# A tuned LoRA kernel on one core: the first two stores wait for the fourth group's projection

## The chip, the core and the metric

The kernel runs on one core of one Trainium2 chip. The core has five engines that run side by side and meet only through semaphores: TensorE (PE, matrix products, with its weight loads as PEld), VectorE (DVE), ScalarE (ACT), GpSimd (POOL) and SyncE (SP). SyncE computes nothing here; it issues every DMA of this kernel. The DMAs are carried out by 16 DMA engines of the core. The metric is the device time of one launch in microseconds (us).

## What is computed

```python
def reference(x, A, B, scale):
    lora = np.matmul(np.matmul(x, A), B)
    return (x + scale * lora).astype(np.float32)
```

x is 16 x 512 x 768 in float32 (25.2 MB), A is 768 x 16, B is 16 x 768, scale is 0.5. The output has the shape of x. So 25.2 MB are read and 25.2 MB are written, and two thin matrix products stand between.

## The kernel before

The 8192 rows of x are cut into 64 tiles of 128 rows. PARTS = [8, 8, 16, 16, 16] (L14) puts the tiles into five parts; inside a part each SBUF partition holds consecutive rows, so that a partition's piece of a transfer is one contiguous row of 6 to 48 KB. The SBUF tensor x_sb has room for 48 tiles, the first four parts; part 4 reuses the places of parts 0 and 1 (L103, modulo ROOM).

The work goes in 8 groups of 8 tiles (GROUP). For a group g:

- ScalarE and GpSimd each cast half of the group to float16, x_sb to xn (L182). For g over 0 they first wait for the load and for s_taken to reach g (L181).
- VectorE transposes xn to xt in one instruction (L238).
- TensorE projects: 24 matmuls into ps_yt (L269). The second of them adds one to s_taken (L277), and no one takes from that counter: its value says how many groups TensorE has begun to project.
- ScalarE spreads the projected values, times scale, into y_bd (L226).
- TensorE multiplies with B into one of two PSUM buffers lora_ps, two tiles at a time ("pairs", four in a group, L290).
- VectorE adds lora_ps to x_sb in place (L243), pair by pair. The sum that completes a store's tiles adds one to s_sum; any other frees its PSUM buffer by s_free.

The order of the instructions on each engine is written out by hand, one function per engine. TensorE interleaves the second product of group g with the projection of group g+1.

SyncE's list sets the order of all DMAs (L135 to L170): loads 0 and 1, the small A and B, loads 2 to 5 (all of them at once, with no wait in between), then the stores of parts 0 and 1, each after a wait for its sum, then loads 6 and 7, each after a wait for one of these stores to land (they fill the same SBUF places), then stores 2, 3 and 4, each after its sum. When SyncE has seen a sum that completes a store, it also frees the PSUM buffer of the group's last pair in VectorE's place (L145). The loads are

```python
LOADS = [
    (0, 0, 2), (0, 2, 6), (1, 0, 8), (2, 0, 8), (2, 8, 8), (3, 0, 16), (4, 0, 8), (4, 8, 8)
]
```

as (part, first tile, tiles). The first six bring 48 tiles, 18.9 MB; load 5 alone is 6 MB. The stores are one per part.

Of the kernel before, what the change touches and what calls it, by code (L numbers as in the profile page):

```python
# [28 lines left out]
def kernel(  # L29
# [53 lines left out]
    def sem(name):  # L83
        sems.append(nc.alloc_semaphore(name))
        return sems[-1]
# [10 lines left out]
    def memory(t2, i, s, n):  # L96
        S = PARTS[i]
        return t2[ds(parts[i], S * P), :].rearrange("(p s) d -> p s d", s=S)[:, ds(s, n), :]

    def held(i, s, n):  # L100
        return tiles(where.index((i, s)), n)

    def tiles(t, n):  # L103
        return x_all[:, ds(t % ROOM, n), :]
# [14 lines left out]
    s_first, s_narrow, s_turned, s_taken = sem("s_first"), sem("s_narrow"), sem("s_turned"), sem("s_taken")  # L119
# [8 lines left out]
    STORES = [(0, 0, 8), (1, 0, 8), (2, 0, 16), (3, 0, 16), (4, 0, 16)]  # L128
# [6 lines left out]
    def on_sync(e):  # L135
        def load(k):
            ld = LOADS[k]
            e.dma_start(out=held(*ld), in_=memory(x2, *ld)).then_inc(s_load[k], 16)  # L138

        def store(k, done):  # L140
            st = STORES[k]
            e.wait_ge(s_sum, k + 1)
            if STORED[k] + 1 < NG:

                e.sem_inc(s_free[PAIRS - 1], 1)  # L145
            e.dma_start(out=memory(out2, *st), in_=held(*st)).then_inc(done, 16)

        load(0)
        load(1)
        e.wait_ge(s_ready, 1)  # L150
        blocks = A.rearrange("(c e) r -> c (e r)", e=64)
        for c in range(SETS):
            e.dma_start(
                out=a_rows[c : SET * SET : SET, :], in_=blocks[ds(c * SET, SET), :]
            ).then_inc(s_a, 16)
        e.wait_ge(s_brows, 1)
        e.dma_start(out=b_rows[0 : R * APART : APART, :], in_=B).then_inc(s_b, 16)
        for k in range(2, len(LOADS) - 2):
            load(k)

        for p in range(2, PAIRS):
            e.sem_inc(s_free[p], 1)
        store(0, s_out0)
        store(1, s_out1)
        e.wait_ge(s_out0, 16)
        load(len(LOADS) - 2)
        e.wait_ge(s_out1, 16)
        load(len(LOADS) - 1)
        for k in range(2, len(STORES)):
            store(k, s_out)  # L170

    here = set()
# [88 lines left out]
    def on_tensor(e):  # L261
# [57 lines left out]
        for p in range(PAIRS):  # L319
            raised(p)  # L320

    on_sync(nc.sync)
    on_gpsimd(nc.gpsimd)
    on_scalar(nc.scalar)
# [46 lines left out]
```

## Time and profile before

| what | value |
|---|---|
| median of 3 runs | 124.05 us (123.84 to 124.35) |
| the profiled execution | 124.01 us, of which the span is 122.2 us |
| DMA queue | one, 1928 packets, 50.43 MB, 96.7% of 16 engines' span |
| VectorE busy | 81.7 us (67%) |
| TensorE busy | 52.3 us (43%) |
| ScalarE, GpSimd busy | 37.4 us, 28.4 us |
| first store issued, landed | 32.82 us, 55.59 us |
| second store issued | 42.74 us |
| load 6 issued, landed | 55.61 us, 70.20 us |
| last store issued | 101.2 us |

The span runs from the first to the last instruction; the measured time holds a little more around it. The slices of the page cut the span in 40 parts of 3.05 us, and a digit is the busy share in tenths. "SPq" rows are SyncE's instructions, and a DMA row of the chain of waits reaches from the issue to the landing, so that time in the queue is in it. A DMA moves one packet per partition here, 128 in all and 8 for each DMA engine, and after its packets each DMA engine writes a small mark (4 bytes) that raises the semaphore; the packet counts of a window split by size, so the marks can be told from the data.

### The profile page before, as it was taken

The page shows a single profiled execution, that of the slowest core. Times are in us where ns is not written, and L with a number is a line of the kernel's source. Part 1 is how long each engine was busy: PE and PEld are TensorE (multiplying, and loading weights), DVE is VectorE, ACT ScalarE, POOL GpSimd, SP SyncE. Part 2 cuts the span into 40 slices and gives each one's busy share as a digit, 9 for nine tenths or more (in the row PEclk, how much of TensorE's full clock was granted, in tenths as well). Part 3 has the DMA queues.
Part 4 walks back from the last instruction along what each step waited for, and adds up shares of the span by engine and source line. Part 5 has one row for each costly group of instructions (what it writes and reads, how often), then busy time and mean ns, then how long its engine had stood idle before and what let it go on. Part 6 is the DMA issues. An engine that isn't in the chain of part 4 may idle for free.

```text
span 122.2 us, 885 instructions
## 1 busy us (share of the span) xinstructions
PE 52.3 (43%) x322; PEld 30.4 (25%) x322; DVE 81.7 (67%) x42; ACT 37.4 (31%) x43; POOL 28.4 (23%) x24
## 2 busy tenths in 40 slices
PE   0000239487457547746745735974674340000000
PEld 0000026253233424424423322642442110000000
DVE  0002850599999999999999979999995991000000
ACT  4002938526408311835340093553004000000000
POOL 7631638026008001705300080440000000000000
PEclk9999999999999999999999996799999955555555
DMA  3999999999998996999999999999899899899890
GB/s 60 420 434 428 451 426 410 459 418 418 483 515 354 418 515 257 467 410 434 442 410 451 426 418 491 426 499 418 370 499 418 370 499 434 354 515 434 386 467 0
DMA packets 1928, 50.43 MB, mean 413 GB/s; under 512 B 236, under 2 KB 236, under 8 KB 392
## 3 DMA queue, kind: packets, MB, share of 16 engines
q1 hardware_dynamic: 1928, 50.43, 96.7%
HBM read 25.26 MB, written 25.17 MB: 413 GB/s over the span
## 4 chain that ended last, share of the span: by engine, by line
DMA 39%; DVE 28%; PE 7%; ACT 3%; issue 3%; POOL 2%; SPq 0%; DVEq 0%
DMA x_sb<-in_x_dram 20%; DMA out_dram<-x_sb 19%; DVE x_sb L243 18%; DVE xt L238 10%; PE ps_yt L269 5%; ACT xn L182 3%; POOL xn L182 2%; PE lora_ps L290 1%; SPq L138 0%; SPq L366 0%; DVEq L256 0%; SPq L145 0%; SPq L133 0%
## 5 line engine op out<-in xcount | busy, mean ns | idle before, releaser
L243 DVE TENSOR_TENSOR x_sb<-x_sb,lora_ps 128x1536 f32<-128x1536 f32 x32 | 53.7, 1733 | 1.4 <-PE lora_ps L290 1.4
L290 PE MATMUL lora_ps<-b_mm,y_bd 128*128 128x512 f16 (+1 forms) x128 | 26.5, 343 | 22.7 <-issue 15.0
L182 ACT CAST xn<-x_sb 128x3072 f16<-128x3072 f32 (+1 forms) x9 | 23.4, 2609 | 36.8 <-DMA x_sb<-in_x_dram 24.2
L238 DVE STREAM_TRANSPOSE xt<-xn 128x3072 f32<-128x3072 f32 (+1 forms) x9 | 27.0, 3004 | 6.7 <-PE ps_yt L269 5.5
L269 PE MATMUL ps_yt<-xt,w_bd 128*128 128x256 f16 x192 | 26.5, 291 | 11.5 <-DVE xt L238 11.5
L182 POOL CAST xn<-x_sb 128x3072 f16<-128x3072 f32 (+1 forms) x8 | 20.7, 2586 | 45.9 <-DMA x_sb<-in_x_dram 23.3
L269 PEld LDWEIGHTS ps_yt<-xt,w_bd 128*128 128x128 f16 x192 | 19.2, 102 | 19.5 <-issue 14.6
L290 PEld LDWEIGHTS lora_ps<-b_mm,y_bd 128*128 128x128 f16 x128 | 11.1, 100 | 36.0 <-issue 18.1
L226 ACT ACTIVATE y_bd<-ps_yt 32x256 f16<-32x256 f32 x32 | 12.0, 374 | 18.3 <-PE ps_yt L269 18.0
L231 DVE STREAM_TRANSPOSE a_t<-a_rows 32x1024 f32<-32x1024 f32 x1 | 1.9, 1945 | 11.4 <-DMA a_rows<-in_A_dram 11.4
L302 PE MATMUL lora_ps<-b_half,pick 128*128 128x512 f16 (+1 forms) x2 | 0.8, 504 | 12.6 <-POOL b_half L200 12.6
L302 PEld LDWEIGHTS lora_ps<-b_half,pick 128*128 128x128 f16 x2 | 0.1, 102 | 12.6 <-issue 12.6
L208 POOL COPY w_bd<-w_one 32x384 f16<-32x384 f16 x4 | 2.0, 500 | 0.2
L200 POOL CAST b_half<-b_rows 128x768 f16<-128x768 f32 x1 | 0.8, 827 | 4.4 <-DMA b_rows<-in_B_dram 4.4
L182 ACT ACT_TABLE_LOAD x1 | 1.3, 1283 | 0.9 <-SPq L133 0.9
L190 POOL MEMSET w_bd<- 128x1536 f32 x1 | 1.4, 1372 | 0.0
L202 POOL CAST w_one<-a_t 32x384 f16<-32x384 f32 x1 | 0.9, 852 | 0.9 <-DVE a_t L231 0.9
L187 POOL MEMSET a_rows<- 32x1024 f32 x1 | 0.9, 941 | 0.5 <-SPq L133 0.5
L219 ACT CAST b_mm<-lora_ps 128x768 f16<-128x768 f32 x1 | 0.8, 798 | 0.0
L188 POOL MEMSET b_rows<- 128x768 f32 x1 | 0.7, 727 | 0.0
L191 POOL MEMSET y_bd<- 128x512 f32 x1 | 0.5, 514 | 0.0
L193 POOL TENSOR_SCALAR_AFFINE_SELECT pick<-pick 128x128 f16<-128x128 f16 x1 | 0.3, 298 | 0.0
(5 smaller groups left out, 0.6 us busy)
## 6 DMA issues: line engine op xcount, KB each, us to landing
out_dram<-x_sb SPq DMA_DIRECT2D x3, 6144.0 KB, 23.6
x_sb<-in_x_dram SPq DMA_DIRECT2D x5, 3072.0 KB, 14.6
x_sb<-in_x_dram SPq DMA_DIRECT2D x1, 6144.0 KB, 42.2
out_dram<-x_sb SPq DMA_DIRECT2D x2, 3072.0 KB, 21.5
x_sb<-in_x_dram SPq DMA_DIRECT2D x1, 2304.0 KB, 9.9
x_sb<-in_x_dram SPq DMA_DIRECT2D x1, 768.0 KB, 4.7
a_rows<-in_A_dram SPq DMA_DIRECT2D x3, 16.0 KB
b_rows<-in_B_dram SPq DMA_DIRECT2D x1, 48.0 KB, 7.5
```

What stands on the lines that cost most here:

```text
L182: ins = copy(out=xn[:, ds(first, n), :], in_=tiles(t, n))
L187: e.memset(a_rows[0:Q], 0.0).then_inc(s_ready, 1)
L190: e.memset(w_bd.rearrange("p c k m -> p (c k m)").bitcast(fp32), 0.0)
L202: e.tensor_copy(out=w_one.rearrange("i (c e) k r -> i c e (k r)", c=SETS), in_=a_t[0:Q].rearrange("i k r (e c) -> i c e (k r)", c=SET)[:, ...
L208: e.tensor_copy(out=w_bd[ds(b * Q, Q), :, :, ds(b * Q, R)], in_=w_one).then_inc(s_w, 1)
L226: last = e.mul(out=y_bd[q, :, q], in_=y_ps[q, :, :], mul=sc)
L231: e.transpose(out=a_t[0:Q].rearrange("i k r c -> i (k r) c"), in_=a_rows[0:Q].rearrange("c (i k r) -> c (k r) i", k=2, r=R),).then_inc(s_r ...
L238: return e.transpose(out=ts[0], in_=ts[1])
L243: ins = e.tensor_tensor(out=xs, in0=xs, in1=lora[p % 2], op=mybir.AluOpType.add)
L269: mm = e.matmul(y_ps, w_bd[:, c, k, :], xv[:, :, c, :, k], start=(m == 0), stop=(m == MMS - 1),)
L290: mms.append(e.matmul(t[:, k, ds(n0, w)], y_bd[:, 2 * p + k, :], b_mm[:, ds(n0, w)], start=True, stop=True,))
L302: last = e.matmul(lora[0][:, 0, ds(n0, w)], pick.rearrange("p b r -> p (b r)"), b_half[:, ds(n0, w)], start=True, stop=True,)
```

## The change

SyncE's helper for a store is split in two: `summed(k)` waits for the sum and frees the PSUM buffer, `store(k)` only issues. For stores 0 and 1 the two waits come first, then a new wait for s_taken to reach 4, that is for the second projecting matmul of the fourth group (g = 3), and then both stores are issued one after the other. The later stores keep their order: wait, free, issue. No other engine's instructions change.

```diff
+        def summed(k):
+            e.wait_ge(s_sum, k + 1)
+            if STORED[k] + 1 < NG:
+
+                e.sem_inc(s_free[PAIRS - 1], 1)
+
         def store(k, done):
             st = STORES[k]
-            e.wait_ge(s_sum, k + 1)
-            if STORED[k] + 1 < NG:
-
-                e.sem_inc(s_free[PAIRS - 1], 1)
             e.dma_start(out=memory(out2, *st), in_=held(*st)).then_inc(done, 16)
 
         load(0)
...
         for p in range(2, PAIRS):
             e.sem_inc(s_free[p], 1)
+        summed(0)
+        summed(1)
+
+
+        e.wait_ge(s_taken, 4)
         store(0, s_out0)
         store(1, s_out1)
         e.wait_ge(s_out0, 16)
...
         load(len(LOADS) - 1)
         for k in range(2, len(STORES)):
+            summed(k)
             store(k, s_out)
```

More of the change, by code (lines that the diff above doesn't have):

```diff
@@ L138, in load @@
             e.dma_start(out=held(*ld), in_=memory(x2, *ld)).then_inc(s_load[k], 16)
-        def store(k, done):
-            st = STORES[k]
+        def summed(k):
             e.wait_ge(s_sum, k + 1)
@@ L145, in store @@
                 e.sem_inc(s_free[PAIRS - 1], 1)
+        def store(k, done):
+            st = STORES[k]
             e.dma_start(out=memory(out2, *st), in_=held(*st)).then_inc(done, 16)
```

## The prediction

> **What bounds the kernel now.** I read the page's 40 slices first, then the queues, then the chain that ended last, and last the DMA packets around the place where the stores are issued.
>
> ```profile
> DVE  0002850599999999999999979999995991000000
> ...
> DMA  3999999999998996999999999999899899899890
> ...
> q1 hardware_dynamic: 1928, 50.43, 96.7%
> ```
>
> From the second slice to the last but one the 16 DMA engines are full, and one queue carries all of it (packets, MB, share). VectorE, the busiest other engine with 67%, ends its last sum at 94.43 + 6.75 = 101.2 us, twenty before the end. So the time is the length of the DMA stream: a start, 50.43 MB at full rate, and any hole in it. Next, the chain of waits, from the first store on:
>
> ```profile
> 32.75 0.02 SPq L145
> 32.77 0.05 issue
> 32.82 22.77 DMA out_dram<-x_sb
> 55.59 0.02 issue
> 55.61 14.59 DMA x_sb<-in_x_dram
> ```
>
> The first store is issued at 32.82 and landed at 55.59, 22.8 us for 3 MB that take 7.3 at full rate. It stood in line. The packets of four short windows show where (columns: packets, MB, and the time the packets took as a share of 16 engines over the window):
>
> ```profile
> q1 hardware_dynamic: 110, 5.41, 99.8%
> ...
> q1 hardware_dynamic: 16, 0.79, 202.0%
> ...
> q1 hardware_dynamic: 16, 0.79, 242.5%
> ...
> q1 hardware_dynamic: 34, 0.44, 104.5%
> ```
>
> The first is 34.0 to 46.9 us: 110 packets of 5.41 MB are 49 KB each, the rows of the 6 MB load, and no store packet is among them although a store has been queued since 32.8 and a second since 42.7. The queue is first in, first out. The fourth is 47.0 to 47.99: 34 packets, of which that answer counts 16 under 512 B (one finishing mark per DMA engine) and the other 18 carry 24.6 KB. So each of the 16 engines ends the last load and begins the first store inside this one microsecond, at 47.0 to 48.0, with nothing lost between. The second and third are 42.9 to 43.8 and 44.7 to 45.6, the last but one and the last 49 KB packet of every engine in that load: 2.020 x 16 x 0.9 / 16 = 1.82 us each, and 2.425 x 0.9 = 2.18 us. The last packets of the load are stretched by 0.36 us on average. That is the only visible flaw of the stream after its start, and the only thing that the queued stores could be blamed for.
>
> **The change, part by part.** SP's two counter steps for group 0 and 1 (L145, at 32.75 and 42.7) stay where they were, since the new helper does them ahead of the new wait: TensorE gets lora_ps buffers as before, cost 0. The two store instructions move from 32.82 and 42.73 to behind a wait for s_taken = 4, the second projecting matmul of the fourth group. Its time:
>
> ```profile
> 36.15 0.38 PE L269 MATMUL ps_yt<-xt,w_bd 128*128 128x256 f16 x2 [1.41 <-DVE xt L238]
> 36.62 2.75 ACT L182 CAST xn<-x_sb 128x3072 f16<-128x3072 f32 x1 [3.44 <-PE ps_yt L269]
> 46.07 0.49 PE L269 MATMUL ps_yt<-xt,w_bd 128*128 128x256 f16 x3 [1.42 <-DVE xt L238]
> 48.34 2.75 ACT L182 CAST xn<-x_sb 128x3072 f16<-128x3072 f32 x1 [5.25 <-DMA x_sb<-in_x_dram]
> ```
>
> One group earlier two matmuls take 0.38 us and ScalarE's cast, which waits for the same counter, starts 0.09 later. So the counter reaches 4 at 46.07 + 0.38 = 46.45 and SP issues the first store at about 46.5, the second 0.4 later. Nothing before that time hangs on a store, so 46.07 itself stays. Behind the wait on SP stand the two stores and then the waits for them to land; SP has nothing else until 55.61.
>
> So the first store now reaches the queue when some engines have 0.5 us of load left and others 1.5. What decides is how long an issued DMA takes to its first packets in an empty queue. The trace has one such place, the first load of the kernel:
>
> ```profile
> 0.96 0.38 SPq L138 DMA_DIRECT2D x_sb<-in_x_dram  x1
> ...
> q1 hardware_dynamic: 14, 0.09, 100.3%
> ```
>
> Issued at 0.96; the second line is the window 1.9 to 2.45, with 14 first packets, the earliest starting at 1.97, and the last engines follow by about 2.5. So 1.0 to 1.55 us from issue to start. Then the packets are slow: those 14 took 1.003 x 16 x 0.55 / 14 = 0.63 us each, against 0.25 in the window 3.3 to 4.0 (45 packets, 98.8%, so 0.988 x 16 x 0.7 / 45), 0.4 us more on a first packet.
>
> The sum, engine by engine. Stores would start at 46.5 + 1.0 to 46.5 + 1.55 = 47.5 to 48.05, where they now start at 47.0 to 48.0. The end is set by the slowest engine, since each has its fixed rows: by the packets the engine that starts the first store last (47.98) also ends last (120.8). Its start moves by 48.05 - 47.98 = 0.07. Added to it is the slow beginning s. Bounds for s: nothing, if reading SBUF has none of the first load's slowness; and on the other side all of that load: its row of 4.7 us to landing is 5.69 on the clock, less 0.35 from last packet to landing (48.34 against 47.98 above) and 8 packets of 0.25, is 2.4 us from issue to an equivalent start at full rate on its slowest engine, hence 46.5 + 2.4 - 47.98 = 0.9 us in all, and s = 0.85. I take the middle, 0.45: the first load read cold from HBM, the store reads from SBUF. Sum +0.07 + 0.45 = +0.5 us.
>
> Does a hole of that size reach the end? Load 6 is issued when store 0 lands, behind store 1 with 7.4 us of packets (55.61 to 63.0), so no second hole opens; all later DMAs shift together. The cast of group 6 (at 70.25, after load 6) shifts along, VectorE ends 0.5 later, and the last store is issued at 101.7 while the store ahead of it, issued at 83.20 with the median 23.6 us to landing, holds the queue to 106.8: cover of over 2 us stays. So the hole is paid in full, once. Gain side: if the queued stores cause the 0.36 us stretch, the loads end earlier by it, but the engines then wait for the stores, which come at 47.5 anyway; group 4's cast at 48.34 would be earlier too, and VectorE does not wait for it now (it is busy without a gap from 25 to 70 us). That gain is covered: 0.
>
> The profiled run took 124.01 us around a span of 122.2; the median of three is 124.05. So 124.01 + 0.5, on the median's scale 124.55.
>
> **A rule of the Trainium skill.** The row says 1.0 us from issue to the first packet. The Trainium skill, DMA: Bandwidth & Descriptors, Specifications, gives a first-byte latency of about 0.6 us for DMAs issued by SyncE; counted from the issue that would be an estimate of a store start at 47.1, almost hidden, and 124.05 in all; the trace agrees with 0.6 only if counted from the end of the issuing instruction (0.96 + 0.38 to 1.97). The same page, Rules for kernel authors, says to issue a DMA early so that its fixed setup overlaps; that speaks against the change, and it is the hole reckoned above.
>
> **The rivals.**
> - *Clearly slower.* The stores pay the first load's whole beginning, s of 0.85 or a little more: 124.05 + 0.07 + 0.85 = 125.0. For it: the only empty queue in the trace behaved so. Against it: there 16 engines waited for cold HBM reads of 6 KB rows; here the rows are 24.6 KB in SBUF. From s of 0.55 on, it is slower by over 0.5%.
> - *Hidden anyway.* s near 0 and a start 0.4 earlier than the first load shows: most engines are still busy with load when the store's packets come. 124.05, no change. For it: 46.5 is before 47.0 for all engines. Against it: 1.0 us of latency.
> - *Faster.* One mechanism: the queued store stretches each engine's last load packet; without it the loads end 0.36 us earlier (on the engine at 47.98 even 0.8, since its packet took 2.66), and the store's packets come within 0.6 us of the issue, by 47.1 to 47.4 (the latest of the load's last packets starts at 45.6, and 45.6 + 1.82 is 47.4). Then the slowest engine gains 47.98 - 47.4 = 0.58: 123.45. It decides only from a start below 0.9 us after issue. Against it: the first load's 1.0 to 1.55.
> - *Not what it says.* At 46.5 the last load still has 0.5 to 1.5 us to go, so the stores do get queued behind loads, only briefly; and 99.8% in the window 34.0 to 46.9, with both stores waiting, shows no slowing there to win back. This caps the gain at what the last packets of the load can give back.
>
> **How the numbers follow.** Forecast +0.2 to +0.8 us around 124.55: 0.52, of which I put 0.15 above the 0.62 us that are 0.5% (about what a measurement of this kernel can tell from no change). Clearly slower, +0.8 and more: 0.25. Hidden, within 0.2 either way: 0.15. Faster: 0.08, of which 0.05 by over 0.5%, as 0.58 is its middle and short of the line. So slower 0.15 + 0.25 = 0.40, faster 0.05, same 0.55. The range goes from 123.9, which leaves out the faster cases, to 125.2, the upper bound of 125.0 and the spread of the three runs (0.2) over it; some 2 in 10 lie outside.
>
> **What would show it.** Right: SP issues the first store near 46.5; the DMA row falls below full for about half a microsecond at 47 to 48.5, and packets of 24.6 KB begin there from 47.5 on; the store lands near 56.1 instead of 55.59, and everything after it is shifted alike. The stretch step is shown by the mean of the last 49 KB packets, 2.18 us or 1.82. Wrong: if store packets begin at 47.1, or if the stores' landing moves by more than 1 us, or if the later DMAs do not shift with it.

## The result and the profile after

The changed kernel takes 125.37 us (median of 12 runs, 124.29 to 126.35) against 124.06 us of the kernel before: a ratio of 1.0096, 95% interval [1.0079, 1.0113]. It is slower by about 1%, and it has become uneven: its runs lie 2 us apart, those of before 0.5. (The ratio leaves out the one run that lies over 1.5% above the kernel's fastest.) On another occasion the same kernel took 124.61 us against 124.11, ratio 1.0037 [1.0019, 1.0054], with runs from 124.10 to 126.03. So it is slower on both occasions, but the size of the loss (1.3 and 0.5 us) is not fixed. The traced run took 125.63 us with a span of 123.8, so it is a typical one of the first twelve.

SyncE's own rows tell most of it, since load 6 is issued when store 0 has landed and load 7 when store 1 has. First the kernel before, then the changed one (start, time, engine, line, what):

```profile
55.61 7.77 SPq L138 DMA_DIRECT2D x_sb<-in_x_dram  x2
63.50 0.36 SPq L146 DMA_DIRECT2D out_dram<-x_sb  x1
```

```profile
46.37 0.82 SPq L148 DMA_DIRECT2D out_dram<-x_sb  x2
55.26 8.50 SPq L138 DMA_DIRECT2D x_sb<-in_x_dram  x2
63.89 0.37 SPq L148 DMA_DIRECT2D out_dram<-x_sb  x1
```

The stores are issued at 46.37. Store 0 has landed at 55.26, 0.35 us *earlier* than before. Store 1 has landed when the second instruction of the pair begins: 63.04 before (55.61 + 7.77 less its 0.34), 63.42 after. So between the two landings 0.73 us were lost. Store 2's row in the list of DMA issues of each kernel (KB, us from issue to landing) gives the rest:

```profile
out_dram<-x_sb SPq DMA_DIRECT2D x1, 6144.0 KB, 28.7
```

```profile
out_dram<-x_sb SPq DMA_DIRECT2D x1, 6144.0 KB, 30.0
```

It lands at 92.2 before and 93.9 after, 1.7 later. Stores 3 and 4, read in the same way (23.7 and 20.2 us after), land at 108.4 and 122.9, against 106.8 and 121.3: 1.6 later. So the change gains 0.35 us up to 55 us, loses 2 us between 55 and 94, and nothing more after that. The loss is nowhere near the place that was changed.

The packets show the two places. In the changed kernel's DMA windows (packets, MB, packet time as a share of 16 engines over the window), in order: 44.8 to 45.7, the last packets of load 5; 46.6 to 47.2; and 47.1 to 47.6, the first packets of store 0.

```profile
q1 hardware_dynamic: 16, 0.79, 202.2%
...
q1 hardware_dynamic: 12, 0.00, 1.1%
...
q1 hardware_dynamic: 22, 0.39, 187.1%
```

The last packets of load 5 take 2.022 x 0.9 = 1.82 us: the stretch of 0.36 us that they had before is gone. Then 12 engines write their mark and nothing else begins until 47.2: a pause like the one predicted, 0.2 us on average. All 16 begin store 0 between 47.2 and 47.5 (16 of the 22 packets are data), and those first packets take 1.871 x 0.5 x 16 / 16 = 0.94 us, as good as the usual 0.91. SyncE waits for the marks of all 16 engines (`wait_ge(s_out0, 16)`), and it is the last of them that gained. By the packet records they end store 0 within 0.24 us of each other, where they lay 0.95 apart before; the average engine ends it at 54.63, against 54.67 before, so it has gained next to nothing. Now the packets ahead of the two later turns: 60.9 to 61.25, the last of store 1 before load 6; then 75.4 to 76.1, the last but one of load 7 before store 2.

```profile
q1 hardware_dynamic: 16, 0.39, 469.6%
...
q1 hardware_dynamic: 16, 0.39, 224.2%
```

4.696 x 0.35 = 1.64 us and 2.242 x 0.7 = 1.57 us, in place of 0.91. In the kernel before, the same two sets (windows 60.66 to 61.57, with 15 of the packets and a mark, and 74.28 to 75.19) take 0.9:

```profile
q1 hardware_dynamic: 16, 0.37, 94.2%
...
q1 hardware_dynamic: 16, 0.39, 100.3%
```

I call the change of the queue from loads to stores, or back, a turn. There are three: at 47, 61 and 76 us. The kernel before pays at the first one and hardly at the others (at 76 us 0.05 on average, 0.26 on the engine that ends last); the changed one pays at the second and third, more in all, and by amounts that differ from run to run.

### The profile page after: what moved, and what is told of

Its sections match the earlier page's. It is cut to its first block, busy times and chain, and to the rows that moved or that the text cites. A ratio compares the mean times of both kernels' runs of the same rounds, so it can differ in the third digit from the quotient of the medians.

```text
span 123.8 us, 885 instructions
## 1 busy us (share of the span) xinstructions
PE 52.6 (43%) x322; PEld 30.8 (25%) x322; DVE 81.8 (66%) x42; ACT 37.5 (30%) x43; POOL 28.4 (23%) x24
## 4 chain that ended last, share of the span: by engine, by line
DVE 49%; PE 13%; issue 9%; DMA 8%; ACT 3%; SPq 0%
DVE x_sb L251 32%; DVE xt L246 18%; PE ps_yt L277 8%; DMA x_sb<-in_x_dram 8%; PE lora_ps L298 5%; ACT xn L190 3%; SPq L138 0%; SPq L374 0%; SPq L133 0%
## 5 line engine op out<-in xcount | busy, mean ns | idle before, releaser
L298 PE MATMUL lora_ps<-b_mm,y_bd 128*128 128x512 f16 (+1 forms) x128 | 26.1, 339 | 23.4 <-issue 14.2
L277 PE MATMUL ps_yt<-xt,w_bd 128*128 128x256 f16 x192 | 27.2, 296 | 11.5 <-DVE xt L246 11.5
L277 PEld LDWEIGHTS ps_yt<-xt,w_bd 128*128 128x128 f16 x192 | 19.6, 104 | 19.9 <-issue 14.6
L298 PEld LDWEIGHTS lora_ps<-b_mm,y_bd 128*128 128x128 f16 x128 | 11.1, 100 | 36.5 <-issue 18.8
## 6 DMA issues: line engine op xcount, KB each, us to landing
out_dram<-x_sb SPq DMA_DIRECT2D x3, 6144.0 KB, 23.7
```

The lines of the kernel that those rows point to most:

```text
L277: mm = e.matmul(y_ps, w_bd[:, c, k, :], xv[:, :, c, :, k], start=(m == 0), stop=(m == MMS - 1),)
L298: mms.append(e.matmul(t[:, k, ds(n0, w)], y_bd[:, 2 * p + k, :], b_mm[:, ds(n0, w)], start=True, stop=True,))
```

## The experiments

In what follows the "extra" of a turn is the time of packets above the usual 0.91 us (24.6 KB) or 1.82 us (49.2 KB), summed over the last three packets ahead of the turn and the first two behind it, as a mean over the 16 DMA engines; it comes from the packet records of each trace. The "lead" is the time from the issue of the store that stands first in the queue to the moment when the first DMA engine ends load 5. A negative or very small lead means a pause. Both are those of the traced run; the lead differs from run to run, since the moment of the issue does (45.24 to 46.37 us in four traces of the changed kernel).

The extra tells where packets are stretched, but it does not give the time: that is set by the DMA engine that ends last, and the extra is a mean. The kernel before has 0.43 us in all, e1 0.7, and both take about 124.1.

| kernel | median, us | lead, us | extra at 47 | at 61 | at 76 |
|---|---|---|---|---|---|
| before | 124.05 | 14.2 | 0.38 | 0 | 0.05 |
| changed | 125.37 | 0.3, pause of 0.2 | 0 | 0.94 | 0.91 |
| changed, second trace | 124.61 (this run 125.80) | 0.9 | 0 | 0.67 | 1.0 |
| changed, third trace | one run, 126.07 | 1.2 | 0 | 0.4 | 1.0 |
| changed, fourth trace | one run, 125.52 | 0.2, pause of 0.3 | 0 | 0.8 | 1.2 |
| e1, third group | 124.15 | 4.7 | 0.7 | 0 | 0 |
| e2, second store only | 124.15 | 14.6 | 0.6 | 0 | 0 |
| e3, load 5 late | 125.71 (this run 124.77) | 16.1 | 1.0 | 0 | 0 |
| e5, pause between stores | 126.04 | 14.6 | 0.8 | 0.9 | 0.9 |
| e6 and f1, tenth pair | 123.62, 123.76 | 2.8, 2.0 | 0.1, 0 | 0.1, 0.1 | 0.5, 0.4 |
| e7, after load 5 | 126.70 | pause of 1.8 | 0 | 0.8 | 1.0 |
| e8, load 5 in halves | 124.16 | 15.3 | 0.7 | 0 | 0 |
| e9, late at every turn | 124.26 (this run 124.05) | 3.1 | 0.3 | 0.1 | 0.5 |
| e10, changed, late turns | 124.87 (this run 124.43) | 1.1 | 0 | 0.24 | 1.0 |
| e11, ninth pair | 124.14 (this run 124.74) | 2.6 | 0.1 | 0.15 | 0.7 |
| f2, early sliver | 123.93 | 14.5 | 0.5 | 0.05 | 0.4 |

Two theories stood against each other at first. HOLE, that of the prediction: the pause at 47 us is what costs. STEP: the pause lets all 16 DMA engines begin store 0 in step (they began 0.95 us apart before, 0.28 apart after the change), and DMA engines in step get in each other's way at the later turns.

### e1: the wait alone

```diff
-        e.wait_ge(s_taken, 4)
+        e.wait_ge(s_taken, 3)
```

> The changed kernel with s_taken >= 3 in place of 4: both stores are issued when the third group's projection begins (36.5 us in the trace of before), well ahead of the end of load 5, so the queue never runs empty. Only the wait itself and the issue of both stores together are left of the change. Theory STEP (the short empty queue at 47 us lets all 16 DMA engines begin store 0 in step, and DMA engines in step are slowed at the later turns between stores and loads): no empty queue, so the time of before, 124.05 within 0.2; the last packets of load 5 stretched by about 0.36 us as before, no packets stretched at 61 or 76 us. Theory HOLE (of the prediction: the loss is the pause itself): also 124.05. Theory TOGETHER (the two stores being issued back to back, or later, costs something at the stores): about 125.3 as the changed kernel.

Measured: 124.15 us, ratio 1.0002 [0.9992, 1.0011]. The stores were issued at 42.48, not at 36.5 as I had written: the wait for the sum of store 1 comes last there. The wait costs nothing, nor does issuing both stores together. What is left of the change is their lateness, which begins to cost at some point between 42.5 and 46.4.

### e2: only the second store late

```diff
         summed(0)
+        store(0, s_out0)
         summed(1)
         e.wait_ge(s_taken, 4)
-        store(0, s_out0)
         store(1, s_out1)
```

> Store 0 is issued as before (32.8 us) and only store 1 waits for s_taken >= 4 (46.5 us). Store 0 stands behind load 5 and covers the issue of store 1. STEP and HOLE: no pause in the DMA stream, 124.05 within 0.2. If the lateness of store 1 alone were the cause: above 124.7.

Measured: 124.15 us, ratio 1.0002 [0.9992, 1.0012]. A late DMA that has another one in the queue ahead of it was free here.

### e3: a thin queue among the loads

```diff
         for k in range(2, len(LOADS) - 2):
+            if k == len(LOADS) - 3:
+                e.wait_ge(s_y, 2)
             load(k)
```

(on the kernel before; SyncE's two counter steps for lora_ps move ahead of the loop)

> The kernel before, with one wait added in another place: load 5 is issued only when s_y reaches 2 (31.6 us), about 0.9 us before the first and 1.2 before the last DMA engine run out of load 4 packets (32.1 to 32.9). The stores are issued as early as before. STEP: a pause of some 0.2 us per DMA engine on average, after which all begin load 5 within 0.3 us of each other; then packets are stretched by about 0.7 us at the next turns (load 5 to store 0 at 47, and perhaps store 1 to load 6), and the time is 124.5 to 125.5. HOLE: only the pause, 124.05 to 124.3, with the stretch at 47 us unchanged at about 0.36. If the late stores themselves are the cause: 124.05 to 124.3.

Measured: 125.71 us, ratio 1.012 [1.0079, 1.016], runs from 124.67 to 127.12. The traced run was one of the shortest, 124.77. Load 5 was issued at 30.6, 1.4 us ahead of the first engine, so the pause that was intended did not come: every engine went from load 4 to load 5 without a gap. Load 5's first packets took 0.23 us more on average, and the extra at the next turn is 1.0 us, the largest at that turn in any trace; none at the later two. HOLE would give no more than 0.23, and STEP had named a pause as its condition and 124.5 to 125.5 as the time. In this trace a queue that nearly ran dry is paid for later, and here the stores were as early as ever. What the longer runs of this kernel paid, no trace shows.

### e4: an uneven store 0

```diff
-        store(0, s_out0)
+        n = 0
+        for p0, np_, s0, ns in ((0, 128, 0, 7), (0, 80, 7, 1), (80, 24, 7, 1), (104, 8, 7, 1),
+                                (112, 8, 7, 1), (120, 4, 7, 1), (124, 4, 7, 1)):
+            q = ds(p0, np_)
+            e.dma_start(
+                out=memory(out2, 0, s0, ns)[q], in_=held(0, s0, ns)[q]
+            ).then_inc(s_out0, 16)
+            n += 16
         store(1, s_out1)
-        e.wait_ge(s_out0, 16)
+        e.wait_ge(s_out0, n)
```

> The changed kernel with store 0 cut so that the same bytes are shared out unevenly: seven tiles as one DMA over 128 partitions, the eighth tile (128 rows of 3 KB) in six DMAs that give DMA engines 0 to 3 eleven rows, 4 to 7 nine, 8 to 11 seven and 12 to 15 five. So after store 0 the engines, which began it in step, stand 0.7 us apart (0.23 per step of four engines), at a cost of 0.34 us for the slowest. STEP: no or much less stretch at 61 and 76 us, so the 0.9 + 0.9 us of the changed kernel are won back but for the 0.34: 123.4 to 124.3, against 125.37 for the changed kernel. HOLE or any theory in which it doesn't matter when the engines stand to each other: 125.4 to 125.8.

Measured: 127.01 us, ratio 1.0237 [1.0222, 1.0252]. This run can't be used for what it was made for. SyncE needed 0.9 to 1.2 us for each of the last five pieces and 1.4 for store 1 behind them, so that store 1 came late in its turn:

```profile
46.32 6.59 SPq L174 DMA_DIRECT2D out_dram<-x_sb  x7
52.95 1.39 SPq L148 DMA_DIRECT2D out_dram<-x_sb  x1
```

Store 1's issue ends at 54.34, and the DMA engines began it between 54.9 and 56.3, some after a second pause. The extras at 61 and 76 are there again (0.8 and 0.9 by its packets).

### e5: the pause at a place where nothing turns

```diff
         summed(0)
+        store(0, s_out0)
         summed(1)
-        e.wait_ge(s_taken, 4)
-        store(0, s_out0)
+        e.wait_ge(s_lora, 14)
         store(1, s_out1)
```

> Store 0 is issued as before, queued behind load 5, so that the turn from loads to stores at 47 us is that of the kernel before. Store 1 waits until TensorE has filled 14 pairs (54.6 us), a little too late: store 0 ends on the DMA engines at 54.3 to 55.25, store 1's packets can begin at about 55.4. So a short empty queue like that of the changed kernel (0.2 us for the last engine, 0.7 on average), but between two stores, where nothing turns. STEP (an empty queue sets the DMA engines in step, and in step they are slowed at later turns): packets stretched at 62 us (store 1 to load 6) by 0.5 to 0.9 us on average and perhaps again at 77; 125.3 to 126.3. Theory FIRST TURN (what costs is that the turn from load 5 to store 0 itself falls into an empty queue): no stretch at 62 and 77 us; only the pause, 124.2 to 124.6.

Measured: 126.04 us, ratio 1.0162 [1.0133, 1.0191], in the range that STEP gave. SyncE's rows of this kernel:

```profile
32.67 22.12 SPq L148 DMA_DIRECT2D out_dram<-x_sb  x2
55.82 8.64 SPq L138 DMA_DIRECT2D x_sb<-in_x_dram  x2
```

Store 0 is issued at 32.67 and store 1 ends its issue at 54.79. The first turn is that of the kernel before (extra 0.8). The pause between the two stores is 0.36 us on average; store 1 then lands 8.3 us after store 0 (64.12 against 55.82), where it takes 7.4 before, and the extras at 61 and 76 are 0.9 and 0.9. So the harm does not depend on the first turn, or on store 0 being late. An empty queue some 8 us ahead of the next turn is enough.

### e6 and f1: the stores two microseconds earlier

```diff
-        e.wait_ge(s_taken, 4)
+        e.wait_ge(s_lora, 10)
```

> The changed kernel, but both stores are issued when TensorE has filled ten pairs (44.7 us) in place of 46.4. Store packets can then begin at about 45.6, a microsecond before the first DMA engine has finished load 5 (46.6). STEP and FIRST TURN: no empty queue, so the stretch of load 5's last packets (0.4 to 0.7 us on average) is back, no stretch at 61 and 76 us, 124.05 to 124.3. If lateness itself costs (the less ahead the stores are issued, the more): between 124.3 and 125.4.

> The kernel of e6_tenth_pair once more, on another occasion: 123.4 to 124.3 with the median near 123.7 if its gain belongs to the kernel; about 124.2, like e11_ninth_pair and e9_late_at_every_turn, if it belonged to that occasion.

Measured: 123.62 us, ratio 0.9969 [0.9952, 0.9985], and on another occasion 123.76, ratio 0.9976 [0.996, 0.9993]. Neither theory had foreseen a gain. This version beats the kernel before on both occasions, by 0.3 and 0.2%, both on the same chip; it is not even either, with runs from 123.41 to 124.53. In the trace of f1 the stores are issued at 44.56 and the first DMA engine ends load 5 at 46.58; no pause, no extra at 47, 0.06 at 61 and 0.39 at 76. So the first turn is without its stretch, the second without harm, and the third takes back by the mean what the first gave: 0.67 us in all for e6 and 0.45 for f1, against 0.43 before. The traces show a gain only in the engine that ends last: it writes its last mark at 120.55 (e6, a run of 123.61) and 120.75 (f1, one of its longer runs, 123.95), against 120.82 before. Where the 0.3% come from is not settled beyond that.

### e7: a longer pause

```diff
-        e.wait_ge(s_taken, 4)
+        e.wait_ge(s_load[5], 16)
```

> The changed kernel, but both stores are issued only when load 5 has landed (about 47.9 us), so the pause is longer: store packets from about 48.8 in place of 47.2 to 47.5. STEP: the engines start store 0 just as much in step, so the same stretches follow (0.9 and 0.9 us on average) and the time is that of the changed kernel and the longer pause, 125.4 + 1.3 to 1.6 = 126.7 to 127.0. HOLE (the pause alone sets the loss): 125.4 + 1.3 to 1.6 as well, but without stretches, which the changed kernel had. If the pause lets the DMA engines recover in some way: below 126.4.

Measured: 126.70 us, ratio 1.0196 [1.0183, 1.0209], in the range that both theories gave; the runs lie within 0.2 us. The pause is 1.78 us on average, and the extras are 0.8 and 1.0, the same as with a pause of 0.2 or 0.3, as STEP had it. The last packets of store 1 in this kernel (window 62.2 to 62.6):

```profile
q1 hardware_dynamic: 16, 0.39, 401.9%
```

4.019 x 0.4 = 1.61 us each. So the long pause brings the same extras as the short one, and its own length on top: 1.33 us more than the changed kernel for a store issued 1.35 us later (47.72 against 46.37). That the two agree so well is partly luck, since the changed kernel's own median was 0.76 us lower on another occasion.

### e8: smaller packets before the turn

```diff
-    (3, 0, 16), (4, 0, 8), (4, 8, 8)
+    (3, 0, 8), (3, 8, 8), (4, 0, 8), (4, 8, 8)
...
-    STORES = [(0, 0, 8), (1, 0, 8), (2, 0, 16), (3, 0, 16), (4, 0, 16)]
+    STORES = [(0, 0, 8), (1, 0, 8), (2, 0, 16), (3, 0, 8), (3, 8, 8), (4, 0, 16)]
```

(on the kernel before; the store of the same tiles, issued after all three turns, is halved with it)

> The kernel before with load 5 (16 tiles) cut into two loads of 8 tiles, so that the packets before the turn at 47 us are 24.6 KB in place of 49.2 KB (0.91 us in place of 1.82); the order and the bytes are the same, the stores are issued early as before. Theory OVERLAP (the stretch arises while a DMA engine is at the last packet of one direction and already reads for the next; a longer packet keeps more of the 16 engines in that state at once): the stretch falls from 0.37 us to 0.1 or less, 123.6 to 123.9. If the stretch belongs to the first turn whatever the packets: unchanged, 124.05.

Measured: 124.16 us, ratio 1.0000 [0.9991, 1.0009]. The extra at 47 us was 0.7, now mostly on the last but one packet of each engine, which ends about 0.9 us ahead of the turn. Shorter packets did not make the stretch smaller; OVERLAP falls.

### e9 and e10: late at every turn

```diff
         e.wait_ge(s_out0, 16)
+        e.wait_ge(s_narrow, 10)
         load(len(LOADS) - 2)
...
             summed(k)
+            if k == 2:
+                e.wait_ge(s_narrow, 12)
             store(k, s_out)
```

(e9 on the kernel of e6, e10 on the changed kernel)

> Both stores at ten pairs as in e6_tenth_pair (123.62), and the same at the two later turns: load 6 is issued not at 55 but when group 5 has been cast (59.2 us, turn at 61.5 to 62.5), store 2 not at 63.5 but when group 6 has been cast (73.0, turn at 75.9 to 77). The queue never runs empty. Theory ADVANCE (packets before a turn are stretched only if the DMAs of the other direction already stand in the queue more than some two us ahead): no stretch at any turn, all runs near 123.3, none above 123.7. Theory STEP alone (the stretch depends only on how far the engines stand apart, 0 at a standard deviation of 0.3 us and 0.9 us at 0.06): as e6_tenth_pair, 123.4 to 124.3.

> The changed kernel (stores at the fourth group, a short empty queue, DMA engines in step) with load 6 and store 2 issued late as in e9. ADVANCE: no stretch at 61 and 76 us though the engines are in step: 0.9 and 0.9 us won back, 123.5 to 124.0 against 125.4. STEP alone: stretched as in the changed kernel, 125.0 to 125.7.

Measured: e9 124.26 us, ratio 1.0026 [1.0000, 1.0051]; e10 124.87, ratio 1.0072 [1.0058, 1.0086], beside 124.61 for the changed kernel on the same chip. SyncE's rows of e10:

```profile
45.34 0.82 SPq L148 DMA_DIRECT2D out_dram<-x_sb  x2
58.13 4.70 SPq L138 DMA_DIRECT2D x_sb<-in_x_dram  x2
72.46 10.59 SPq L148 DMA_DIRECT2D out_dram<-x_sb  x2
```

What was forecast from ADVANCE did not come: no run of e9 lies below 123.7, and in e10 store 2 was issued at 72.5, where the changed kernel has it at 63.9, and the extra at 76 is 1.0 all the same. But its condition was not met. In e10 the first engine reaches the turns at 61.4 and 77.1, so load 6 and store 2 still stood in the queue 3.3 and 4.6 us ahead; in e9 it is 3.1 us at each turn. All of that is more than the two us of the theory, so whether a lead under two us would spare the later turns was not tested. At 47 us the traces go with it: the extra is 0 to 0.1 with leads up to 2.8 us, 0.3 with 3.1 (e9) and 0.7 with 4.7 (e1). It can't be all, since in the kernel before load 6 stands 6 us ahead of its turn and nothing is stretched there. At 61 the extra of e10 was 0.24. e9 lies in the range of STEP alone, e10 just below it.

### e11: the ninth pair

```diff
-        e.wait_ge(s_taken, 4)
+        e.wait_ge(s_lora, 9)
```

> Both stores at nine pairs (43.9 us), 0.65 us earlier than e6_tenth_pair. ADVANCE with a limit of some two us before the turn: the stretch of load 5's last packets begins to come back, 123.7 to 124.1, between e6_tenth_pair (123.6) and the kernel before (124.1). If only the fact that they are issued during load 5 matters: as e1_wait_third_group, 124.15.

Measured: 124.14 us, ratio 1.0006 [0.9997, 1.0015]. That is the time of e1, and above what ADVANCE gave. But no trace shows the 0.65 us more of lead: here the stores were issued at 43.87, 2.6 us ahead, and in e6 at 43.80, 2.8 us ahead, so run-to-run differences are as large as the edit. The kernels also ran on different chips. Whether a longer lead took e6's gain away is open; the traced run was the longest of its kernel, so its extras say little of the median.

### e12, f3 and f4: the changed kernel again

> The changed kernel itself once more, to stand beside the others on one chip and for a second trace. 125.37 within 0.5; DMA engines in step after the empty queue, the packets before the turns at 61 and 76 us stretched by 0.7 to 1.0 us on average, and the time of the profiled run above 123.5 by about the sum of the stretches at the two turns.

> A third trace of the changed kernel, to see what goes with a short and what with a long run: no stretch before the turn at 47 us, 0.6 to 1.2 us on average in all before each of the turns at 61 and 76, whether or not the queue ran empty at 47 (it does when SP issues store 0 less than 0.9 us before the first DMA engine ends load 5).

> A fourth trace of the changed kernel, with the same expectation as for f3_changed_look: no stretch at 47 us, 0.6 to 1.2 us in all before each of the turns at 61 and 76.

Measured: 124.61 us, ratio 1.0037 [1.0019, 1.0054], below the 125.37 within 0.5 that was expected; the traced runs took 125.80, 126.07 and 125.52. Other expectations failed too: in the second trace the queue did not run empty, the engines were not in step, and its time lies 2.3 us above 123.5 with 1.7 us of extra; the third has 0.4 at 61, below 0.6. The third trace settles what the pause is worth. SyncE's rows, and then the DMA windows 46.3 to 47.2 and 75.0 to 76.6:

```profile
45.24 0.82 SPq L148 DMA_DIRECT2D out_dram<-x_sb  x2
54.96 8.01 SPq L138 DMA_DIRECT2D x_sb<-in_x_dram  x2
```

```profile
q1 hardware_dynamic: 32, 0.39, 103.0%
...
q1 hardware_dynamic: 16, 0.39, 77.0%
```

In this run the computation ran about a microsecond ahead of the loads, compared with the first trace, and the stores were issued at 45.24. All 16 marks and all 16 first packets of store 0 lie in the first window, and the engines' packet time fills it: there was no pause. Nor were the engines in step: they began store 0 over 0.77 us. And yet the 16 packets that begin in the second window, ahead of the turn at 76, took 0.770 x 1.6 = 1.23 us each in place of 0.91, and the run is the longest of the four. Its mean extra of 1.4 us is the smallest of the four, though. The packets that begin from 121.0 us on (window 121.0 to 124.2) show why:

```profile
q1 hardware_dynamic: 2, 0.05, 3.6%
```

They are one packet and one mark: a single DMA engine is still at work and ends at 123.02, when the other 15 have ended by 120.96, which is close to the 120.82 of the kernel before. In the second trace it is one engine too, with 122.74 against 121.55. In the first and fourth, with a pause, most engines are late: the average one ends at 121.9 and 122.0, against 120.1 before. So neither HOLE nor STEP, as they stood, is right. What the four traces share is a queue that held no more than 1.2 us of work for the first DMA engine when the stores were issued. Why one engine then falls behind the rest in two of them stays open.

### f2: a sliver early

```diff
         summed(0)
+        e.dma_start(out=memory(out2, 0, 0, 1), in_=held(0, 0, 1)).then_inc(s_out0, 16)
         summed(1)
         e.wait_ge(s_taken, 4)
-        store(0, s_out0)
+        e.dma_start(out=memory(out2, 0, 1, 7), in_=held(0, 1, 7)).then_inc(s_out0, 16)
         store(1, s_out1)
-        e.wait_ge(s_out0, 16)
+        e.wait_ge(s_out0, 32)
```

> The changed kernel, but one tile of store 0 (3 KB rows, an eighth of its bytes) is issued early, at 32.8 us, and stands behind load 5; the other seven tiles and store 1 are issued at s_taken >= 4 as in the change. The sliver keeps each DMA engine busy for about 1 us after load 5, until the rest is there. Theory FIRST TURN STRETCHED (what spares the later turns in the kernel before is that load 5's last packets were stretched, because a store stood behind them early): stretch of 0.4 to 0.8 us at 47, none at 61 and 76, 124.1 to 124.3. Theory LATE (it is the late issue of the bulk of the stores that spoils the later turns): 124.6 to 125.4, with the stretches at 61 and 76 us of the changed kernel.

Measured: 123.93 us, ratio 0.9982 [0.9974, 0.9991], runs within 0.3 us. SyncE's rows, and the DMA window 44.6 to 45.5, the last packets of load 5:

```profile
32.59 0.35 SPq L166 DMA_DIRECT2D out_dram<-x_sb  x1
46.25 0.34 SPq L169 DMA_DIRECT2D out_dram<-x_sb  x1
46.64 0.43 SPq L148 DMA_DIRECT2D out_dram<-x_sb  x1
55.37 7.82 SPq L138 DMA_DIRECT2D x_sb<-in_x_dram  x2
```

```profile
q1 hardware_dynamic: 16, 0.79, 253.6%
```

The bulk of the stores is issued as late as in the changed kernel (46.25 against 46.37), and only one tile, 0.4 MB, is early. That is enough: 2.536 x 0.9 = 2.28 us for the last packets of load 5, so the stretch at 47 is back (0.5), at 61 there is 0.05, at 76 0.4, and the 1.3 us of the change are undone. LATE falls; FIRST TURN STRETCHED is right at 47 and 61, but not about 76, and the time is below its range. The sliver gives the queue 1 us more of work behind load 5 when the bulk arrives: the lead of the bulk over the first engine's end of the sliver is 48.0 - 46.25 = 1.8 us.

## Why the prediction was wrong, point by point

- *The DMA stream sets the time.* Right: 0.35 us gained and 2 us lost in the stream end up as 1.6 us in the span, with the last store issued 5.7 us before the store ahead of it has landed (102.7 against 108.4).
- *SyncE issues the stores at 46.5; the counter steps cost nothing; nothing moves before.* Right for the first trace: 46.37, and e1 shows wait and counters to be free. Three further traces of the same kernel have 45.24 to 46.31, and from 45.6 on down there is no pause at all; the prediction took the time of one trace as fixed.
- *Store packets from 47.5 to 48.05, a slow beginning of 0.45, +0.5 us.* Wrong in size and in sign. They began 0.84 us after the issue, at 47.2 to 47.5, and were not slow (0.94 us against 0.91). The term was worth -0.35 us at store 0's landing. The 0.45 was taken from the first load of the kernel, which did not stand for a store; what made that load's first packets slow, no run shows. The Trainium skill gives about 0.6 us of first-byte latency (DMA: Bandwidth & Descriptors, Specifications). This trace shows 0.84 from the issue, between that and the 1.0 I took, and 0.49 from the end of the issuing instruction.
- *The stretch of load 5's last packets: its loss is covered, 0.* Right for the average engine, wrong for the last. The 0.36 us came back, but the pause took 0.2 of it and the average engine ends store 0 at 54.63, against 54.67 before. The engine that is last, and so the landing, gained 0.35.
- *"So no second hole opens; all later DMAs shift together"; "So the hole is paid in full, once".* This is the step that failed. No second hole to speak of opened, but the packets themselves became longer: 0.94 us on average at the turn at 61 and 0.91 at 76. The text treated the transfer rate behind the pause as fixed. The profile of before shows packets that are stretched ahead of a turn, and I took that as one flaw at one place, "the only visible flaw". There was a second, small one: ahead of 76 us the engine that ends last loses 0.26. That a stretch could come at the other two turns was in none of the rivals.
- *The rivals.* "Clearly slower" ended near the right time (125.0 against 125.37), by a mechanism that did not occur, so its nearness is luck. "Faster" had the mechanism of the first half right: without early stores the stretch at 47 goes, and e6 has that and 123.62. It lacked the price (and its sum, 124.05 - 0.58, is 123.47 and not 123.45).
- *What would make it wrong.* The text named it: the later DMAs do not shift along with store 0.

The same page of the Trainium skill says to issue a DMA early, so that its fixed setup overlaps (Rules for kernel authors). The runs agree that too late costs: 124.15 with a lead of 4.7 us, 125.37 with 0.3, though most of that cost was not the setup. How early, the page does not say; here 123.62 with a lead of 2.8 beats 124.15 with 4.7, on another chip.

**What is shown and what is not.** Shown: the loss lies in longer packets ahead of the turns at 61 and 76, on most engines in the traces with a pause and far more on one than on the others in two without (e12, f3); a pause brings it, a short and a long one (changed, e7) and at two places (e5); the pause itself costs about its own length, 0.2 us in the changed kernel; without a pause, a lead of 0.9 to 1.2 us brings it too (e12, f3, e10); with a lead of 2 us or more, or a sliver that fills the queue, it is nearly gone at 61 (at most 0.15) and 0.4 to 0.7 us are left at 76 (e6, f1, f2, e9, e11). Not shown: what in the chip remembers a short queue for 15 to 30 us. It is not how far apart the engines stand alone, as I first thought: f1 and e12 both begin store 1 with a standard deviation of 0.20 and 0.19 us between the engines, and have 0.06 and 0.67 us of extra at 61. Nor is it the packet size (e8) or the lateness of the stores as such (e2, f2). How far ahead the next DMA is queued may have a part in it: no experiment brought the later turns under two us (e9, e10). Why one stretched turn at 47 spares the kernel before the other two stays open as well.

## What to carry to other kernels

Where the DMA queue is the bound, a wait that delays an issue must be weighed against how much work the queue still holds at that moment, and a microsecond was too little here; with two to three us the kernel stayed within 0.3% of the time of before, on either side. If a late issue is wanted, a small DMA of the same kind in the queue ahead of it was enough here (f2). And a sum over a DMA stream should not end at the first hole: compare the landing of each later transfer, since the price can come 15 us after its cause, and look at the DMA engine that ends last and not at the average alone.

## What the runs showed of the hardware that I had not expected

- A change of one queue between loads and stores can stretch the packets just ahead of it, by up to 1.2 us in all on the average DMA engine, or not at all; in the kernel before one of three turns costs 0.4 us.
- One DMA engine of the 16 can end 2 us behind all others, though each large DMA gives every engine the same 8 packets (f3: 123.02 against 120.96 for the next), and the kernel takes its time from that one.
- The stretched packets begin some 1.6 to 2.7 us ahead of the turn; with half as long packets (e8) most of the stretch was on the last but one. Behind the turn little of it was seen: load 6's first packets took 1.03 us in the changed kernel, in place of 0.91.
- DMAs over 24, 8 and 4 partitions took SyncE 0.9 to 1.2 us each to issue while the queue was busy, and the full store behind them 1.4 (e4), where a store over 128 partitions takes 0.34 to 0.43 otherwise.
- An idle queue had its first store packets under way 0.84 us after the issue, with no slow first packet; the first load of the kernel took 1.0 us and had packets 0.4 us too long.
